# Attention operands filled up to 128 rows, values at columns 0 and 96, and the heads' norms split between VectorE and GpSimd

## The chip, the core and the metric

The kernel runs on one core of one Trainium2 chip. A core has a matrix engine (TensorE, PE in the profile; its weight loads are listed apart as PEld and overlap the matmuls), VectorE (DVE), ScalarE (ACT), GpSimd (POOL) and SyncE (SP), which here only issues DMAs. Each engine works through its own instructions in order, and semaphores tie the engines together. The metric is the device time of one launch in microseconds, as the median of several runs. A change of less than about 0.3% can't be told from none.

## The reference

One layer of a trunk in which three kinds of heads stand side by side: 2048 tokens, width 1024, all in float32.

```python
h = RMSNorm(x); z = h @ W_in + b_in      # columns shared out among the heads
y = concat[ FoX attention (8 heads of 64), mLSTM (4), HGRN2 (4) ]
x = x + y @ W_out
h = RMSNorm(x)
x = x + W_down( silu(conv3(h W_up)_gate) * conv3(h W_up)_up )
```

What the change touches is the attention. Its score of query t and key u, with q and k normed and c the running sum of the log forget gates, is

```python
s = einsum('qd,kd->qk', q, k) / 8 + c[q] - c[k]     # per head
s = where(kpos <= qpos, s, -inf)
o = softmax(s) @ v
y_head = RMSNorm(o) * gain                          # norm over the 64 columns of a head
```

## The kernel before, in words

**Numbers.** A matmul here takes operands of reduced precision (type fp32r). To come near float32, an operand is split into a high part and the low part that is left over, and three matmuls are added up: high by high, high by low, low by high. The helper `mm3` (L198) does this in the projections.

**Stages.** The kernel first makes the projections z and, woven into them, the mLSTM and HGRN2 mixers, in two halves of 1024 tokens. For the attention these write to HBM: the high and low parts of q and k, transposed, with one row for each column of the heads (s_qh, s_ql, s_kh, s_kl); the values (s_v), 130 numbers for a token and head, which are 64 high parts, a one, 64 low parts and a zero; the forget sums (s_fc), and rows of ones and zeros (s_one). The last projections end with stores of s_v and s_qh by GpSimd's queue (L321, L404). Then come the attention, the output projection with the second norm (`phase_out`) and the FFN (`ffn_up`, `ffn_down`), whose large products are made of fewer products of blocks with sums of blocks on VectorE and GpSimd.

**Who sets the order.** Outside the attention's loop a planner of the framework puts the instructions of each engine in order, by a simulated time and by what each one depends on. The loop of the attention stands in `with k.tc.manual_schedule()` (L1006): there each engine keeps the order in which the program names its instructions. Memory is shared between stages: QB and KB of the even heads lie where the first buffer of the projections' high parts was, QA and KA of the even heads where the first buffer of their low parts was, those of the odd heads in the second buffers, and V of the even heads where the low parts of the projection's weights (wlo) were.

**Operands of a head.** `att_load` (L805) issues a head's loads on SyncE, all through one helper (L813), so that all carry its line. QB is 64 rows of the high parts of q and six rows more: four that receive the negated row maxima, and two with ones; KB has the high parts of k, four rows of ones or zeros against the maxima, and two rows of the forget sums. So one matmul with 70 rows gives the high product, plus the forget sums, minus the maximum of the row. QA is q high over q low and KA is k low over k high, 128 rows, so that one more matmul gives both cross products. V is a tile of 128 tokens by 16 by 130.

**The loop.** For each of the 8 heads there are 4 blocks of 512 queries, and for each of them the key tiles of 128 up to the diagonal: 4 + 8 + 12 + 16 = 40 steps for a head. In a step:

- `att_scores` (L876) makes the scores transposed, keys by queries: the matmul with QB and KB (L885), the one with QA and KA (L886), and on the diagonal a mask added by a matmul with the identity. ScalarE makes the exponentials pf (L892) and their high part ph (L894); the low part pl (L898) is a subtraction, in three steps of four on GpSimd, in the fourth on VectorE one step later.
- `att_maxima` (L829) runs ahead, 12 pieces before the first score and then 22: a matmul with QB and KB the other way round (L845), a mask, and a maximum over the row on VectorE (L850). When a block of 512 queries is through, its maxima are transposed and written into rows 64 to 67 of QB (L863).
- `att_values` (L903) runs three steps behind the scores (`SKEW`): V high by ph with the ones column, whose output row 64 is the sum of the softmax (L911), V low by ph (L912), and V high by pl (L913), all added into one PSUM tile. At the end of a block the sum goes through ScalarE and TensorE (transposes) into the tile `o` of the head, with tokens on the rows.
- In the fourth step of each head from the second on, the loads of the head after it are issued.

**A head's norm.** `att_finish` (L937) hands the pieces of a head's norm to `Later` (L787), a list of due steps: `put(n, f)` runs f at the end of the n-th step from now, behind that step's other work. For heads 0 to 6 one norm covers all 16 tiles of 128 tokens and falls into the head after it. From its step 6 on come the reciprocal of the softmax sums (rl), the squares on ScalarE and their totals on VectorE, four tiles a step. In step 11 come two products of the totals with rl (L960, L961) and the start of the inverse root in `rms_steps` (L113): three operations with a constant, then the first of three Newton steps. The other two follow in steps 12 and 13:

```python
nc.vector.tensor_tensor(u, out, out, op=ALU.mult)
nc.vector.tensor_tensor(u, u, h, op=ALU.mult)
nc.vector.scalar_tensor_tensor(out, u, 1.5, out, op0=ALU.add, op1=ALU.mult)
```

All of these work on 128 x 16 numbers. From step 15 the factor is multiplied by rl (L970), and then four tiles a step are multiplied by it on VectorE (L971) and by the gain on GpSimd (L976). SyncE stores the head's columns into s_y (L981). The last head has no head after it: each of its four blocks of queries is normed by itself (128 x 4 numbers), beginning four steps after the block's end.

**Beside it.** The load of the gains `ga` (L1628) belongs to the attention and stands ahead of the loop in the program. The weights of the output projection are loaded and split inside the loop (L1040). `phase_out` reads s_y back by tiles of 128 tokens, all heads together.

## Time and profile before

| | before |
|---|---|
| median of 3 runs | 2932.36 us (2932.19 to 2941.21) |
| the profiled execution | 2937.63 us |
| its span, first to last instruction | 2935.5 us |
| mean granted clock of TensorE | 0.977 |
| TensorE busy | 2817.4 us, 96% of the span |
| VectorE busy | 2005.9 us, 68% |
| GpSimd busy | 1435.1 us, 49% |
| ScalarE busy | 1280.0 us, 44% |

By stage, in us of the span:

| stage | from, to | TensorE busy | VectorE | ScalarE | GpSimd | clock |
|---|---|---|---|---|---|---|
| projections and mixers | 0 to 939 | 880.89 | 596.28 | 278.12 | 373.70 | 0.97 |
| attention | 939 to 1440 | 467.65 | 381.69 | 381.91 | 339.73 | 0.95 |
| output projection | 1440 to 1680 | 227.64 | 129.10 | 74.60 | 40.65 | 0.96 |
| FFN | 1680 to 2935.5 | 1241.22 | 898.81 | 545.33 | 681.07 | 1.00 |

How to read the lines that follow. A line in order of time has the start and the duration in us (with x3 behind it, the sum of three), the engine, the program line, the operation, out<-in by the program's names, shapes, and in brackets how long the engine had waited and for whom. SPq and POOLq are the queues of SyncE and GpSimd, which issue DMAs. A line of the waits names who waited and for whom, then the sum in us, the number of waits and the longest. A line of the stretches has from and to and the length, the busy time of TensorE, its weight loads, VectorE, ScalarE and GpSimd with their instructions, then the granted clock, the share of the DMA engines and GB/s. A line of a group has the busy time and the mean of one instruction in ns, and the idle time ahead of them with what ended most of it.

### The profile page before, as it was taken

To read this page: it belongs to the slowest core of one execution; us is meant where nothing else is said; L and a number is where in the kernel's file an instruction comes from. 1 tells how busy PE (TensorE), PEld (TensorE's weight loads), DVE (VectorE), ACT (ScalarE), POOL (GpSimd) and SP (SyncE) were. 2 spreads that over 40 slices of the span, in tenths; PEclk is the share of its full clock that TensorE was granted. 3 is DMA by queue.
4 is the path that set the end of the run, shared out by engine and by line. 5 is a ranking of instruction groups with operands and counts; after the bars stand their busy time and mean duration, and the time that the engine had idled before them with its cause. 6 is when DMAs were issued, how large, how long until landed. Compare 5 with 4: busy or idle time off the path is not lost. (4 is left out here: it accounts for less than half of the span.)

```text
span 2935.5 us, 42833 instructions
## 1 busy us (share of the span) xinstructions
PE 2817.4 (96%) x15181; PEld 2342.7 (80%) x15181; DVE 2005.9 (68%) x3384; ACT 1280.0 (44%) x2167; POOL 1435.1 (49%) x1199
## 2 busy tenths in 40 slices
PE   7999988999988999999899899999999999999999
PEld 7898987889988666666688788888788888888887
DVE  7337687265786787778546577677797577777655
ACT  4213323132322778878424344444454343444443
POOL 2245452334454577766302366666475644444443
PEclk9999997999999999999999999999999999999999
DMA  4424434333334554342257444444777333333666
GB/s 159 127 93 133 150 96 143 94 108 97 111 107 143 107 114 88 81 92 49 72 179 246 148 155 151 154 148 158 268 247 271 114 108 108 108 105 117 232 214 209
DMA packets 346615, 411.07 MB, mean 140 GB/s; under 512 B 47650, under 2 KB 234096, under 8 KB 343232
## 3 DMA queue, kind: packets, MB, share of 16 engines
q1 hardware_dynamic: 292016, 318.45, 37.2%
q10 hardware_dynamic: 51952, 81.45, 7.6%
q0 software_dynamic: 2432, 8.42, 0.8%
q8 instruction: 120, 1.97, 0.3%
q14 instruction: 95, 0.78, 0.1%
HBM read 280.24 MB, written 127.98 MB: 139 GB/s over the span
## 5 line engine op out<-in xcount | busy, mean ns | idle before, releaser
L1221 POOL TENSOR_TENSOR w<-w,w 128x512 fp32r<-128x512 f32 x302 | 404.8, 1353 | 403.3 <-ACT w L1220 339.2
L1409 PE MATMUL ps<-w,w 128*128 128x512 f32 x1848 | 420.9, 389 | 4.0 <-ACT w L1400 2.0
L1409 PEld LDWEIGHTS ps<-w,w 128*128 128x128 f32 x1848 | 346.6, 188 | 77.6 <-ACT w L1400 2.4
L198 PE MATMUL w<-whi,hhi 128*128 128x256 f32 (+1 forms) x1280 | 370.4, 289 | 3.1 <-DVE lr L1766 2.0
L198 PE MATMUL w<-whi,hlo 128*128 128x256 f32 (+1 forms) x1280 | 371.3, 290 | 0.0
L198 PE MATMUL w<-wlo,hhi 128*128 128x256 f32 (+1 forms) x1280 | 370.4, 290 | 0.6 <-POOL wlo L189 0.6
L898 POOL TENSOR_TENSOR pl<-pf,ph 128x512 fp32r<-128x512 f32 (+2 forms) x240 | 287.8, 1212 | 146.6 <-ACT ph L894 133.3
L1402 POOL TENSOR_TENSOR w<-w,w 128x512 fp32r<-128x512 f32 x154 | 216.3, 1412 | 200.9 <-ACT w L1400 155.4
L1220 ACT ACTIVATE w<-w 128x512 fp32r<-128x512 f32 x302 | 180.4, 627 | 258.7 <-POOL w L1221 86.7
L850 DVE TENSOR_REDUCE mx<-m 128x1 f32<-128x512 f32 (+2 forms) x320 | 190.8, 605 | 91.3 <-PE m L845 63.1
L1401 DVE TENSOR_TENSOR w<-w,w 128x512 fp32r<-128x512 f32 x154 | 179.9, 1178 | 103.4 <-ACT w L1399 102.0
L198 PEld LDWEIGHTS w<-whi,hhi 128*128 128x128 f32 x1280 | 245.2, 192 | 4.8 <-issue 3.8
L198 PEld LDWEIGHTS w<-wlo,hhi 128*128 128x128 f32 x1280 | 244.9, 191 | 2.7 <-POOL wlo L189 1.0
L198 PEld LDWEIGHTS w<-whi,hlo 128*128 128x128 f32 x1280 | 244.7, 191 | 1.8 <-issue 0.5
L892 ACT ACTIVATE pf<-s 128x512 f32<-128x512 f32 (+1 forms) x320 | 172.5, 539 | 91.1 <-PE s L886 50.9
L1226 DVE TENSOR_TENSOR w<-w,w 128x512 f32<-128x512 f32 x176 | 149.8, 870 | 85.3 <-DMA w<-in_w_up_dram 81.0
L189 POOL TENSOR_TENSOR wlo<-wraw,whi 128x1024 fp32r<-128x1024 f32 (+1 forms) x56 | 135.3, 2433 | 111.7 <-ACT whi L188 102.2
L894 ACT ACTIVATE ph<-pf 128x512 fp32r<-128x512 f32 (+1 forms) x320 | 185.1, 578 | 10.3
L1267 DVE SCALAR_TENSOR_TENSOR u<-ps,fcol,u 128x1023 f32<-128x1023 f32 x88 | 108.9, 1279 | 95.3 <-ACT u L1266 95.3
L913 PE MATMUL pv<-pl,V 128*65 128x512 f32 (+1 forms) x320 | 121.7, 380 | 25.2 <-DVE pl L898 24.3
L1400 ACT ACTIVATE w<-w 128x512 fp32r<-128x512 f32 x154 | 96.6, 628 | 111.3 <-PE ps L1409 88.7
L1399 ACT ACTIVATE w<-w 128x512 fp32r<-128x512 f32 x154 | 95.9, 623 | 89.8 <-POOL w L1402 44.4
(374 smaller groups left out, 7092.1 us busy)
## 6 DMA issues: line engine op xcount, KB each, us to landing
w<-in_w_up_dram SPq DMA_DIRECT2D x182, 256.0 KB
w<-s_g SPq DMA_DIRECT2D x154, 256.0 KB
w<-in_w_down_dram SPq DMA_DIRECT2D x110, 256.0 KB
wraw<-in_w_in_dram SPq DMA_DIRECT2D x48, 512.0 KB
s_g<-u ACTq DMA_DIRECT2D x88, 256.0 KB
w<-s_w SPq DMA_DIRECT2D x88, 256.0 KB
s_g<-w ACTq DMA_DIRECT2D x66, 256.0 KB
x<-in_x_dram SPq DMA_DIRECT2D x32, 512.0 KB
```

The lines of the kernel that those rows point to most:

```text
L189: nc.gpsimd.tensor_tensor(lo[:, q : q + n, :], raw, h.bitcast(F32), op=ALU.subtract)
L198: nc.tensor.matmul(out, lsl(lhs[a], i), rsl(rhs[b], i), start=(i == 0 and j == 0), stop=(i == n - 1 and j == 2))
L850: nc.vector.tensor_reduce(mx[:, i, kb : kb + 1], m[:, 0:n], axis=AX.X, op=ALU.max)
L892: nc.scalar.activation(pf[:, c0:], s[:, c0:], AF.Exp)
L894: nc.scalar.activation(ph[:, c0:], pf[:, c0:], AF.Copy)
L898: eng.tensor_tensor(pl[:, c0:], pf[:, c0:], ph[:, c0:].bitcast(F32), op=ALU.subtract)
L1220: nc.scalar.activation(h, t, AF.Copy)
L1221: nc.gpsimd.tensor_tensor(lo, t, h.bitcast(F32), op=ALU.subtract)
L1226: nc.vector.tensor_tensor(t, x, y, op=op)
L1401: nc.vector.tensor_tensor(gl, gr, gh.bitcast(F32), op=ALU.subtract)
L1402: nc.gpsimd.tensor_tensor(wl, wr, wh.bitcast(F32), op=ALU.subtract)
L1409: nc.tensor.matmul(tiles[tile], g[x][:, tile * P : (tile + 1) * P], w[y], start=j == 0 and c == 0, stop=j == nj - 1 and c == 2,)
```

## The change

It has four parts.

**128 rows.** The matmuls L845 and L885 take all 128 rows of QB and KB instead of 70. For this QB and KB are no longer made anew for each head: there are two pairs, made once ahead of the loop, and GpSimd fills their rows 64 to 127 with zeros. The call for the first pair, `zero(0)`, stands ahead of the hand-ordered block, the one for the second, `zero(1)`, in it, behind the first head's loads. The loads of ones and forget sums then write rows 64 to 69 as before.

**Columns of V.** The tile has 160 columns for a token tile instead of 130, with the low parts from column 96 on instead of 65 (96 x 4 bytes = 384 = 3 x 128; 160 x 4 = 640 = 5 x 128). The zero column is no longer loaded. High and low parts are loaded by a DMA each, so V takes four DMAs instead of two.

**Order of the loads.** The first part of V was loaded ahead of QA and KA; now all of V comes behind them.

**The norm.** The two products with rl, the three Newton steps and the product of the factor with rl go from VectorE to GpSimd. A Newton step has four operations there instead of three. The three operations with a constant at its start stay on VectorE. In the last head the quarters begin 18, 10, 4 and 4 steps after their blocks' ends instead of 4 each, and they share one tile of 128 x 16 x 64 for the squares and products, where before each had its own of two.

```diff
+VL, VW = 96, 160
...
-def rms_steps(k, pool, out, ss, n, epsf, tag):
+def rms_steps(k, pool, out, ss, n, epsf, tag, pool_too=False):
...
     for _ in range(3):
         yield
+        if pool_too:
+            nc.gpsimd.tensor_tensor(u, out, out, op=ALU.mult)
+            nc.gpsimd.tensor_tensor(u, u, h, op=ALU.mult)
+            nc.gpsimd.tensor_scalar(out=u, in0=u, scalar1=1.5, scalar2=None, op0=ALU.add)
+            nc.gpsimd.tensor_tensor(out, out, u, op=ALU.mult)
+            continue
...
@@ def att_load(k, h, st):
-    QA, KA, QB, KB = (k.t(k.pat[f"{t[1]}{h % 2}"], [P, T], F32R, tag=t) for t in ("QA", "KA", "QB", "KB"))
-    V = k.t(k.pat[f"V{h % 2}"], [P, 16, 130], F32R, tag="V")
+    QA, KA = (k.t(k.pat[f"A{h % 2}"], [P, T], F32R, tag=t) for t in ("QA", "KA"))
+    QB, KB = k.qkb[h % 2]
+    V = k.t(k.pat[f"V{h % 2}"], [P, 16, VW], F32R, tag="V")
...
     ld(KB[68:70], k.s_fc[h])
-    v = k.s_v[:, h, :].rearrange("(jt p) c -> p jt c", p=P)
-    ld(V[:, 0:4], v[:, 0:4])
     ld(QA[0:64], k.s_qh[r])
     ld(QA[64:128], k.s_ql[r])
     ld(KA[0:64], k.s_kl[r])
     ld(KA[64:128], k.s_kh[r])
-    ld(V[:, 4:16], v[:, 4:16])
+    v = k.s_v[:, h, :].rearrange("(jt p) c -> p jt c", p=P)
+    for j in (slice(0, 4), slice(4, 16)):
+        ld(V[:, j, 0:65], v[:, j, 0:65])
+        ld(V[:, j, VL : VL + 64], v[:, j, 65:129])
...
-                        m[:, 0:nn], QB[0:70, q0 : q0 + P], KB[0:70, kb * BLK : kb * BLK + nn], start=True, stop=not last
+                        m[:, 0:nn], QB[:, q0 : q0 + P], KB[:, kb * BLK : kb * BLK + nn], start=True, stop=not last
...
-    nc.tensor.matmul(s[:, c0:], KB[0:70, js], QB[0:70, qs], start=True, stop=False)
+    nc.tensor.matmul(s[:, c0:], KB[:, js], QB[:, qs], start=True, stop=False)
...
-    nc.tensor.matmul(po[0:64, c0:], V[:, j, 65:129], ph[:, c0:], start=False, stop=False)
+    nc.tensor.matmul(po[0:64, c0:], V[:, j, VL : VL + 64], ph[:, c0:], start=False, stop=False)
...
-        att_finish(k, st, pa, 4 * qb, 4, later, 4)
+        att_finish(k, st, pa, 4 * qb, 4, later, (18, 10, 4, 4)[qb])
...
@@ def att_finish: first()
-        w["sq"] = k.t(pa, [P, n, HD], tag=f"asq{n}", bufs=bufs)
+        if n == 16 or "sq" not in st:
+            st["sq"] = k.t(pa, [P, 16, HD], tag="asq", bufs=1)
+        w["sq"] = st["sq"][:, t0 : t0 + n, :]
...
     def scale():
-        nc.vector.tensor_tensor(w["ss"], w["ss"], w["rl"], op=ALU.mult)
-        nc.vector.tensor_tensor(w["ss"], w["ss"], w["rl"], op=ALU.mult)
+        nc.gpsimd.tensor_tensor(w["ss"], w["ss"], w["rl"], op=ALU.mult)
+        nc.gpsimd.tensor_tensor(w["ss"], w["ss"], w["rl"], op=ALU.mult)
...
-        w["chain"] = rms_steps(k, pa, w["s"], w["ss"], HD, 1.0, f"a{n}")
+        w["chain"] = rms_steps(k, pa, w["s"], w["ss"], HD, 1.0, f"a{n}", pool_too=True)
...
         if c.start == 0:
-            nc.vector.tensor_tensor(w["s"], w["s"], w["rl"], op=ALU.mult)
+            nc.gpsimd.tensor_tensor(w["s"], w["s"], w["rl"], op=ALU.mult)
...
@@ def attention(k, pa, ps, side):
+    k.qkb = [[k.t(k.pat[f"B{i}"], [P, T], F32R, tag=t) for t in ("QB", "KB")] for i in range(2)]
+    def zero(i):
+        for x in k.qkb[i]:
+            k.nc.gpsimd.memset(x[64:128].bitcast(F32), 0.0)
+
+    zero(0)
     with k.tc.manual_schedule():
         att_load(k, 0, sts[0])
+        zero(1)
         att_load(k, 1, sts[1])
```

## The prediction

> **What bounds the kernel now.** I read the page first, then the stretches by stage, the waits of TensorE and the order of time at three places. The attention runs from 939 to 1440 us. TensorE has little idle time anywhere, so what counts is where it waits and where its clock falls.
>
> ```profile
> span 2935.5 us, 42833 instructions
> ```
> ```profile
> 943.10:963.60 20.50, 13.71 (x42) 8.91 (x42) 10.43 (x21) 4.97 (x11) 5.91 (x10) 0.50 0.90 247
> ...
> 1042.00:1045.50 3.50, 3.50 (x10) 2.12 (x10) 3.29 (x8) 1.23 (x2) 2.77 (x4) 0.52 0.00 0
> ...
> 1400.00:1411.00 11.00, 6.99 (x23) 3.96 (x22) 10.00 (x21) 4.08 (x8) 7.63 (x9) 0.69 0.15 36
> ```
> ```profile
> PE pv L913 <- DVE pl L898: 24.3, 15, 4.0
> ```
> The stretches give, behind the five busy times, the granted clock, the DMA share and GB/s. At the start of the attention the clock is 0.50 for 20.5 us. After a wait of TensorE it is about half for a stretch such as 1042 to 1045.5, which costs half of those 3.5 us. In all of the attention TensorE waits 24.3 us for the low parts (pl) that VectorE makes, nearly all of it in eight long waits, one behind each head's end and a second one in the last head. With the clock lost behind them I count 24 + 8 x 1.75 = 38 us. That is the most that the steps on GpSimd could win. The profiled execution took 2937.63 us, 2.1 more than its span, and the median of the runs is 2932.36. I work out differences in the span and add them to the median.
>
> **Loads of the first head: values last, and the zeroed rows.** SyncE's order of time, and its wait:
>
> ```profile
> 916.20 0.51 SPq L1628 DMA_DIRECT2D ga<-in_out_g_dram  x1
> ...
> 918.90 0.26 SPq L813 DMA_DIRECT2D KB<-s_fc  x1
> 939.18 0.39 SPq L813 DMA_DIRECT2D V<-s_v  x1
> ...
> 941.45 0.85 SPq L813 DMA_DIRECT2D KA<-s_kh  x1
> ```
> ```profile
> SPq L813 <- PE w L198: 20.0, 1, 20.0
> ```
> ```profile
> 939.06 0.28 PE L845 MATMUL m<-KB,QB 70*128 70x256 f32 x1
> ...
> 946.82 0.78 PE L885 MATMUL s<-QB,KB 70*128 70x512 f32 x1
> 953.71 0.79 PE L886 MATMUL s<-QA,KA 128*128 128x512 f32 x1 [6.11 <-DMA KA<-s_kh]
> ```
> V's first load waits 20 us for the projection's last matmul, whose memory it takes, and the four loads of QA and KA stand behind it. So the first score, begun at 946.82, gets its second pair at 953.71. With V moved past those four loads they would go at 919, and 953.71 - 946.82 = 6.9 us would be won. But the load of ones into QB[64:70] now waits for the memset of QB's rows 64 to 127, and everything behind it on SyncE (KB's rows, QA, KA, V, the next head's loads) waits with it. When does GpSimd come to that memset?
>
> ```profile
> 904.27 0.59 POOL L321 DMA_DIRECT2D s_v<-h  x1 [0.30 <-POOL h L318]
> ```
> ```profile
> 936.92 0.68 POOL L318 TENSOR_TENSOR h<-z,h 128x256 fp32r<-128x256 f32 x1
> ...
> 940.79 0.71 POOL L404 DMA_DIRECT2D s_qh<-h  x1 [0.35 <-ACT h L317]
> ...
> 950.73 0.10 POOL L315 MEMSET h<- 128x4 f32 x1 [6.58 <-DMA s_qh<-h]
> ...
> 951.89 1.11 POOL L321 DMA_DIRECT2D s_v<-h  x2
> 956.06 1.27 POOL L898 TENSOR_TENSOR pl<-pf,ph 128x512 fp32r<-128x512 f32 x1 [3.07 <-ACT ph L894]
> ```
> ```profile
> s_qh<-h POOLq DMA_DIRECT2D x4, 256.0 KB, 2.8
> ```
> ```profile
> L1578 POOL MEMSET q<- 128x1024 f32 x1 | 1.0, 951 | 0.3 <-POOLq L1807 0.3
> ```
> The zeroing of the first pair stands outside the hand-ordered block, so the planner may put it early. The one instruction with the same place in the program is the load of ga: it needs nothing but an input, yet it was issued at 916.20, behind SyncE's last load of the projections, and GpSimd's first attention step (956.06) stands behind its last store of the projections (951.89). I take it that the memsets come behind that store too. Then SyncE issues no QA or KA loads while the store of 940.79 is under way, and I let it land after its median 2.8 us, at 943.6, before GpSimd asks for it (950.73 - 6.58 = 944.15). From 950.73 to the store's end, 951.89 + 1.11 = 953.00, are 2.3 us, so GpSimd is free at 946.4. A memset of 1024 columns took 0.951 us, so 2048 columns take 1.9 and the pair 3.8: 950.2. The loads of ones and of the forget sums follow and land some 2.8 us on (the store's time as the nearest row), at 953. TensorE's first maximum thus begins 14 us late. The maxima ahead of the first score took 946.82 - 939.06 = 7.8 us, bound by VectorE; they end at 960.8. QA and KA, 2.1 MB issued from 950.8, need 8.5 us at the 247 GB/s of the stretch above, 1.5 more to begin: 960.8 as well. Against 953.71 that is **+7 us**. Bounds: -6.9 if the memsets come early; +14 if the store lands as late as it did before. The second pair's memsets (3.8 us on GpSimd) lie ahead of its first pl, which has nothing to work on by then; without that cover they cost 3.8, inside the upper bound. V goes in four loads, not two: 0.39 us of issue each on a queue that is idle, and V is read three steps after the first score; uncovered, its 260 KB cost 1.1 us at 247 GB/s. Later heads load 35 steps ahead.
>
> **The heads' norms, first seven heads.** A head's end at 1205 to 1220 us, VectorE, GpSimd and TensorE in order of time:
>
> ```profile
> 1210.12 0.18 DVE L132 SCALAR_TENSOR_TENSOR as<-a16u,as 128x16 f32<-128x16 f32 x1
> ...
> 1211.02 0.80 DVE L130 TENSOR_TENSOR a16u<-as 128x16 f32<-128x16 f32 x1
> ...
> 1213.11 1.22 DVE L132 SCALAR_TENSOR_TENSOR as<-a16u,as 128x16 f32<-128x16 f32 x1
> ...
> 1215.94 0.81 DVE L970 TENSOR_TENSOR as<-as,rl 128x16 f32<-128x16 f32 x1
> ...
> 1218.22 1.74 DVE L898 TENSOR_TENSOR pl<-pf,ph 128x512 fp32r<-128x512 f32 x1
> ```
> ```profile
> 1210.27 4.02 POOL L898 TENSOR_TENSOR pl<-pf,ph 128x512 fp32r<-128x512 f32 x3 [1.94 <-ACT ph L894]
> 1215.42 1.29 POOL L898 TENSOR_TENSOR pl<-pf,ph 128x512 fp32r<-128x512 f32 x1 [1.13 <-ACT ph L894]
> ...
> 1217.97 1.44 POOL L898 TENSOR_TENSOR pl<-pf,ph 128x512 fp32r<-128x512 f32 x1
> ```
> ```profile
> 1213.21 0.40 PE L886 MATMUL s<-QA,KA 128*128 128x512 f32 x1
> 1213.45 0.40 PE L845 MATMUL m<-KB,QB 70*128 70x512 f32 x1
> ...
> 1217.27 0.39 PE L912 MATMUL pv<-ph,V 128*64 128x512 f32 x1
> 1220.02 0.69 PE L913 MATMUL pv<-pl,V 128*65 128x512 f32 x1 [2.36 <-DVE pl L898]
> ```
> Alone, a step of the norm takes VectorE 0.18 us; beside GpSimd's pl it takes 0.80 to 1.22, until GpSimd's instruction ends. So the factor of the norm (L970) is ready at 1216.75; VectorE's products and its own pl follow, and TensorE, ready at 1217.5, waits until 1220.
>
> Now the 15 steps of the norm go to GpSimd, twelve of them four by four behind pl of steps 12, 13 and 14, then the last factor. Call one p. GpSimd starts at 1210.27, makes three pl of 1.29 and 13 small ones: the factor is ready at 1214.14 + 13p. VectorE's products wait for it, and its pl stands behind two of them, as before. If VectorE gets in ahead of GpSimd's next pl, product 0.4, reduce 0.65 (covered by that pl, 1.29 from the product on), product 0.35, one gain 0.7 and pl 0.65 follow: 3.05 us, and TensorE waits 13p - 0.3. If GpSimd's pl goes first, 1.29 and 0.3 more are in the way: 13p + 1.3. Before it was 2.5.
>
> p isn't in the trace. From 0.68 us at 256 columns and 1.29 at 512 follows 0.11 at 16 columns; 0.10 for the 128x4 memset says the same. Each step needs the one before, and GpSimd took 0.30 us to begin an instruction on its own result (904.27). So p lies between 0.11 and 0.43; I take 0.22, nearer the low end, because that 0.30 was before a DMA issue. Then TensorE waits 2.55 or 4.15, 3.35 in the mean: **0.9 more than before in each of seven heads, +6 us**. Bounds: p = 0.11 with VectorE first shortens each wait to 1.1 and the clock may hold, -3.2 a head, -22; p = 0.43 with the mean, +3.6 a head, +25.
>
> [...]
>
> **The last head.** Its quarters are normed one by one. Two long waits stand here:
>
> ```profile
> 1395.25 0.33 PE L913 MATMUL pv<-pl,V 128*65 128x256 f32 x1 [3.04 <-DVE pl L898]
> ...
> 1405.11 0.69 PE L913 MATMUL pv<-pl,V 128*65 128x512 f32 x1 [4.01 <-DVE pl L898]
> ```
> The first quarter now begins at step 24 of the head instead of 10, so the second wait (4.0, and 3.4 of the eleven us at clock 0.69) goes: -7. But the second quarter begins at step 24 too, so GpSimd gets eight small steps (8 x 0.22 = 1.8 us) beside a pl of 1.29 in steps of five matmuls, 5 x 0.235 = 1.2 us. Over three such steps it falls 5.6 us behind with some 2.5 us of slack, so TensorE waits about 3 again, and 1.75 for its clock; the first wait grows by 0.9. Sum: **-1, taken as 0**; bounds -6 and +6. The stores of these quarters come at step 33, seven steps (8 us) before the end, and the output projection's first load needs them then; hidden by the last scores, +4 if not.
>
> **128 rows and V's columns: 0.** The matmuls and their number stay.
>
> ```profile
> L885 PEld LDWEIGHTS s<-QB,KB x320: 187/188/353, 946.7 to 1436.6; 70*128 70x128 f32 x160
> ```
> ```profile
> L886 PEld LDWEIGHTS s<-QA,KA x320: 189/191/336, 953.7 to 1436.8; 128*128 128x128 f32 x160
> ```
> ```profile
> L1409 PE MATMUL ps<-w,w 128*128 128x512 f32 x1848 | 420.9, 389 | 4.0 <-ACT w L1400 2.0
> ```
> Weights of 70 and 128 rows load alike (least, median and longest in ns), and the full-row L886 takes 0.24 us to the next start, as the 70-row L845 does. The FFN's matmuls take 420.9 / 1848 = 0.228. If that gap of 0.007 came from rows and columns, some 1700 matmuls would win 12 us: bounds -12 and 0, and I take 0, because L886 has full rows already. Memory moves by 2 KB a head buffer, which no row prices.
>
> **Sum:** +7 + 6 + 0 + 0 = +13, so 2932.4 + 13 = 2945.
>
> **The rivals.**
> *Zeroing early.* The planner puts the first memsets into GpSimd's idle time before 939. For it: the wait of 6.58 and others leave room, and QB's memory was free at 917. Against it: ga. Start -6.9 instead of +7: 2931.
> *The norm gets off VectorE's back (the other side: faster).* The place is the factor's arrival at 1214.14 + 13p, and it decides below p = 0.12, with VectorE getting in first. Waits shrink to about 1.1 us, and I let the clock hold; -22 in seven heads, -6 in the last, start +7: 2911. For it: the 0.10 us memset; against it: each step waits for its predecessor.
> *GpSimd's small steps are dear*, p = 0.35: 13p makes +2.6 a head, +18; last head +5, start +7: 2962.
> *Full rows hold the clock.* The half-clock stretches (14 us behind eight waits, some 5 at the start) go: 2945 - 19 = 2926. For it: 20.5 us at 0.50 while TensorE was mostly on 70-row work; against it: no row ties the clock to rows. [...]
>
> **How the numbers follow.** The forecast has 0.48, with its own range 2936 to 2960. Early zeroing has 0.18, the relief 0.16, the dear steps 0.12, the clock 0.06. About 0.3% (8.8 us) is what a measurement of this kernel tells from no change, so 2923.6 and 2941.2 are the limits. Faster: 0.03 of early zeroing, 0.14 of the relief, 0.03 of the clock, 0.20. Same: 0.10 of the forecast, 0.12 of early zeroing, 0.02 and 0.03, 0.27. Slower: the rest, 0.53. The range 2914 to 2966 leaves out most of the relief and the far end of the dear steps, some 0.17.
>
> **What would show it.** Right: the first maximum near 953 behind two memsets of about 1.9 us, SyncE's load of ones waiting for GpSimd, no wait of TensorE for KA over 2 us; steps of 128x16 on GpSimd at 0.1 to 0.3; waits for pl of 2 to 4 us at every head's end, with half clock behind them. Wrong: memsets before 939 with QA issued by 925; waits for pl under 1.5 us; matmul starts 0.228 us apart.

## The result, and the profile after

| | before | after |
|---|---|---|
| median | 2936.60 us (4 runs) | 2955.68 us (4 runs) |
| ratio | 1 | 1.0075, 95% interval 1.0056 to 1.0093 |
| the profiled execution, its span | 2937.63, 2935.5 us | 2955.15, 2953.4 us |

So the change makes the kernel slower by 0.75%, about 22 us; a second comparison of the same two kernels (first experiment below) gave 1.0079. The forecast was 2945.0, 13 us slower, with its own range 2936 to 2960. Direction and range hold; the sum is 9 us short. (A fourth run moved the median of the kernel before from 2932.36 to 2936.60.) In the last experiment below, one of six executions took 7051 us; its time and ratio are those of the other five.

To see where it went, the table follows seven marks on TensorE in the profiled executions: (a) the last transposition of the projections, (b) the second score matmul of the first step, (c) the same matmul of step 10 of head 0, (d) that of step 10 of the last head, (e) the last transposition of the attention, (f) the first product of the FFN and (g) its last. These are marks b to f of the changed kernel, in order of time:

```profile
958.38 0.77 PE L896 MATMUL s<-QA,KA 128*128 128x512 f32 x1 [2.33 <-DMA KA<-s_kh]
...
975.56 0.28 PE L896 MATMUL s<-QA,KA 128*128 128x256 f32 x1
...
1396.03 0.28 PE L896 MATMUL s<-QA,KA 128*128 128x256 f32 x1
...
1459.64 0.46 PE L935 MATMUL x<-ident,oT 65*128 65x65 f32 x4 [0.68 <-ACT oT L929]
...
1662.79 0.47 PE L1273 MATMUL ps<-b11h,w 128*128 128x512 f32 x1
```

All times are in us. The stretch c to d holds the norms of heads 0 to 5 and d to e those of heads 6 and 7, because a head's norm falls into steps 11 to 18 of the next one. For e the last of its four transpositions counts.

| kernel | a | a to b | b to c | c to d | d to e | e to f | f to g |
|---|---|---|---|---|---|---|---|
| before | 938.47 | 15.23 | 19.02 | 413.55 | 54.80 | 205.57 | 1282.58 |
| after | 934.47 | 23.91 | 17.18 | 420.47 | 63.85 | 202.90 | 1284.28 |
| difference | -4.0 | +8.7 | -1.8 | +6.9 | +9.05 | -2.7 | +1.7 |

Up to a and from f on both kernels run the same work; those two columns differ by 6 us and more among the kernels of this study, which is the scatter of single executions. In the attention the stretches are steadier, but not exact: moving V's loads alone changed c to d by 0.15 us, while the changed kernel run a second time took 423.14 there instead of 420.47. So a difference of less than about 3 us in c to d is not read as an effect below.

**The start** of the changed kernel, in order of time on SyncE, GpSimd and TensorE, and the wait of SyncE:

```profile
943.95 0.30 SPq L822 DMA_DIRECT2D QB<-s_one  x1
945.69 0.27 SPq L822 DMA_DIRECT2D KB<-s_one  x1
...
946.31 0.45 SPq L822 DMA_DIRECT2D QA<-s_qh  x1
...
948.08 0.59 SPq L822 DMA_DIRECT2D KA<-s_kh  x1
```
```profile
940.98 1.11 POOL L329 DMA_DIRECT2D s_v<-h  x2
942.13 1.80 POOL L1023 MEMSET QB<- 64x2048 f32 x1
943.87 1.80 POOL L1023 MEMSET KB<- 64x2048 f32 x1
```
```profile
948.45 0.55 PE L855 MATMUL m<-KB,QB 128*128 128x256 f32 x1 [13.23 <-DMA KB<-s_fc]
```
```profile
SPq L822 <- POOL QB L1023: 29.9, 1, 29.9
```

The memsets stand right behind the last store of the projections, and SyncE waits 29.9 us for the first of them, with all but the first two loads of the first head behind it.

**A head's end.** GpSimd, VectorE and TensorE of the changed kernel, at the same head as in the prediction:

```profile
1217.65 1.29 POOL L908 TENSOR_TENSOR pl<-pf,ph 128x512 fp32r<-128x512 f32 x1 [1.44 <-ACT ph L904]
1218.90 0.21 POOL L130 TENSOR_TENSOR a16u<-as 128x16 f32<-128x16 f32 x1
1219.19 0.22 POOL L131 TENSOR_TENSOR a16u<-a16u,a16h 128x16 f32<-128x16 f32 x1
1219.50 0.25 POOL L132 TENSOR_SCALAR a16u<-a16u 128x16 f32<-128x16 f32 x1
1219.84 0.22 POOL L133 TENSOR_TENSOR as<-as,a16u 128x16 f32<-128x16 f32 x1
1220.02 1.30 POOL L908 TENSOR_TENSOR pl<-pf,ph 128x512 fp32r<-128x512 f32 x1
...
1224.87 0.22 POOL L983 TENSOR_TENSOR as<-as,rl 128x16 f32<-128x16 f32 x1
1225.05 1.27 POOL L908 TENSOR_TENSOR pl<-pf,ph 128x512 fp32r<-128x512 f32 x1
```
```profile
1225.13 1.48 DVE L984 TENSOR_TENSOR asq<-ao,as 128x256 f32<-128x256 f32 x1 [4.63 <-POOL as L983]
1226.53 0.68 DVE L860 TENSOR_REDUCE mx<-m 128x1 f32<-128x512 f32 x1
1227.13 0.56 DVE L984 TENSOR_TENSOR asq<-ao,as 128x256 f32<-128x256 f32 x1
1227.61 1.74 DVE L908 TENSOR_TENSOR pl<-pf,ph 128x512 fp32r<-128x512 f32 x1
```
```profile
1223.73 0.45 PE L923 MATMUL pv<-pl,V 128*65 128x512 f32 x1 [0.64 <-POOL pl L908]
...
1229.41 0.69 PE L923 MATMUL pv<-pl,V 128*65 128x512 f32 x1 [3.81 <-DVE pl L908]
```

A small step takes GpSimd 0.21 to 0.25 us, but they start 0.29 to 0.34 apart, since each needs the one before; two that do not need each other started 0.15 apart in the last head, at 1427.39 and 1427.54. Four of them put the next pl off by 1.12 us. VectorE waits 4.63 us for the factor, with its own pl behind that wait, and TensorE waits 0.64 and 3.81 us where it had waited 2.36.

**The last head**, TensorE, VectorE and GpSimd:

```profile
1431.97 0.45 PE L923 MATMUL pv<-pl,V 128*65 128x512 f32 x1 [1.51 <-POOL pl L908]
...
1435.23 0.69 PE L923 MATMUL pv<-pl,V 128*65 128x512 f32 x1 [1.88 <-POOL pl L908]
...
1438.49 0.69 PE L923 MATMUL pv<-pl,V 128*65 128x512 f32 x1 [0.86 <-POOL pl L908]
...
1444.43 0.69 PE L923 MATMUL pv<-pl,V 128*65 128x512 f32 x1 [3.55 <-DVE pl L908]
```
```profile
1442.37 1.20 DVE L122 TENSOR_SCALAR a4m<-ass 128x4 f32<-128x4 f32 x1 [2.58 <-POOL ass L974]
...
1443.68 0.69 DVE L908 TENSOR_TENSOR pl<-pf,ph 128x512 fp32r<-128x512 f32 x1
```
```profile
1427.10 0.21 POOL L973 TENSOR_TENSOR ass<-ass,rl 128x4 f32<-128x4 f32 x1
...
1430.66 1.26 POOL L908 TENSOR_TENSOR pl<-pf,ph 128x512 fp32r<-128x512 f32 x1
```

Twelve small steps of two quarters, from 1427.10 to 1430.66, hold one pl back by 3.6 us; then the third quarter's totals stand in GpSimd's queue behind a pl, and VectorE's pl behind the wait for them. The stretches of time give the price in clock (behind the five busy times: granted clock, DMA share, GB/s):

```profile
1433.80:1447.50 13.70, 7.86 (x18) 4.44 (x18) 3.17 (x8) 4.12 (x7) 11.93 (x28) 0.50 0.20 59
```

### The profile page after: what moved, and what is told of

Its sections match the earlier page's. It is cut to its first block, busy times and chain, and to the rows that moved or that the text cites. A ratio compares the mean times of both kernels' runs of the same rounds, so it can differ in the third digit from the quotient of the medians.

```text
span 2953.4 us, 42896 instructions
## 1 busy us (share of the span) xinstructions
PE 2809.3 (95%) x15181; PEld 2332.7 (79%) x15181; DVE 1964.4 (67%) x3252; ACT 1279.4 (43%) x2167; POOL 1476.8 (50%) x1368
## 5 line engine op out<-in xcount | busy, mean ns | idle before, releaser
L1241 ACT ACTIVATE w<-w 128x512 fp32r<-128x512 f32 x302 | 180.4, 627 | 256.8 <-POOL w L1242 85.7
L1421 ACT ACTIVATE w<-w 128x512 fp32r<-128x512 f32 x154 | 96.7, 628 | 116.7 <-PE ps L1430 88.5
L855 PE MATMUL m<-KB,QB 128*128 128x512 f32 (+2 forms) x320 | 130.3, 414 | 14.6 <-DMA KB<-s_fc 13.2
```

The source lines that it names most:

```text
L1241: nc.scalar.activation(h, t, AF.Copy)
```

## The experiments

Each kernel was run beside the kernel before; ratios are against it, with 95% intervals. The stretches are those of the table above.

**The changed kernel again.** No edit.

> The changed kernel once more, beside the runs of this set. Both theories: 18 to 24 us slower than before (22 in the first comparison, 17.5 between the two profiled executions, of which the projections, the same instructions in both, took 4 us less).

Measured 2961.38 us against 2936.74, ratio 1.0079 (1.0066 to 1.0092), +23 us. Stretches: a to c 41.2 against 34.25, c to d 423.14, d to e 64.10. As expected.

**The norms back on VectorE.** The changed kernel with

```diff
-        nc.gpsimd.tensor_tensor(w["ss"], w["ss"], w["rl"], op=ALU.mult)
-        nc.gpsimd.tensor_tensor(w["ss"], w["ss"], w["rl"], op=ALU.mult)
+        nc.vector.tensor_tensor(w["ss"], w["ss"], w["rl"], op=ALU.mult)
+        nc.vector.tensor_tensor(w["ss"], w["ss"], w["rl"], op=ALU.mult)
...
-        w["chain"] = rms_steps(k, pa, w["s"], w["ss"], HD, 1.0, f"a{n}", pool_too=True)
+        w["chain"] = rms_steps(k, pa, w["s"], w["ss"], HD, 1.0, f"a{n}")
...
-            nc.gpsimd.tensor_tensor(w["s"], w["s"], w["rl"], op=ALU.mult)
+            nc.vector.tensor_tensor(w["s"], w["s"], w["rl"], op=ALU.mult)
```

> The changed kernel with the norms' steps back on VectorE (due times of the last head as changed). Theory: GpSimd's small steps cost the changed kernel +7 us in seven heads and about +10 in the last, the late zeroing +5 to +8 at the start, rows and columns nothing; so about 5 to 8 us slower than the kernel before, and the changed kernel's other 15 us are gone. Rival (operands: the full rows or V's columns and extra DMAs cost something in every head): still 15 us or more slower than before.

Measured 2937.31, ratio 1.0006 (0.9995 to 1.0018): +2 us, not to be told from none. The theory's 5 to 8 was too high, the rival's 15 is out. In sum, the norms on GpSimd are the loss: without them the later start (a to c 40.02 against 34.25) is balanced by the stretch c to d, which took 407.44, 6 us less than before the change. The operands seem to win something that I had at nothing.

**Only the last head's norms back on VectorE.**

```diff
-        w["chain"] = rms_steps(k, pa, w["s"], w["ss"], HD, 1.0, f"a{n}", pool_too=True)
+        w["chain"] = rms_steps(k, pa, w["s"], w["ss"], HD, 1.0, f"a{n}", pool_too=n == 16)
...
+        e = nc.gpsimd if n == 16 else nc.vector
```

> The changed kernel with only the last head's four small norms back on VectorE. Theory (GpSimd falls behind in the last head, up to twelve small steps in one loop step): 8 to 12 us faster than the changed kernel, about 10 to 14 slower than before; no wait of TensorE for a low part over 1 us in the last 25 us of the attention but those that the last head had before. Rival (it is the due times of the last head, two quarters in the same step, not the engine): no more than 3 us faster than the changed kernel.

Measured 2953.10, ratio 1.0062 (1.0046 to 1.0078). That is 2.6 and 8.3 us faster than the two medians of the changed kernel and, by the ratios, 4 to 5, so less than the theory's 8 to 12; the intervals of these ratios overlap. The stretch d to e is the cleaner reading: 57.50 against 63.85 and 64.10, so the four small norms cost 6.4 us on GpSimd. But the theory's sign, no wait over 1 us in the last 25 us of the attention, failed: one of 4.09 us stands at 1436.97. Two quarters in the same step, the rival's cause, make VectorE late too. The rest of that stretch's loss is the large norm of head 6, which falls into it.

**V behind QA and KA alone.** The kernel before with its two V loads moved behind KA.

```diff
-    v = k.s_v[:, h, :].rearrange("(jt p) c -> p jt c", p=P)
-    ld(V[:, 0:4], v[:, 0:4])
...
     ld(KA[64:128], k.s_kh[r])
+    v = k.s_v[:, h, :].rearrange("(jt p) c -> p jt c", p=P)
+    ld(V[:, 0:4], v[:, 0:4])
     ld(V[:, 4:16], v[:, 4:16])
```

> The kernel before with both loads of V behind QA and KA, nothing else. Theory: QA and KA are issued by 920 instead of after 939, the first score's second matmul no longer waits (6.1 us before), 6.9 us faster: about 2929.5 against 2936.6. Rival (the end of the projections and the maxima set the pace, and the time is lost again at the first read of V): within 2 us of before.

Measured 2930.57, ratio 0.9984 (0.9974 to 0.9995), -5 us. The stretches show 27.76 us from a to c instead of 34.25, -6.5, and nothing elsewhere in the attention: the 6.9 of the prediction within half a us.

**128 rows alone.** The kernel before with the zeroed pairs and full rows.

```diff
-                        m[:, 0:nn], QB[0:70, q0 : q0 + P], KB[0:70, kb * BLK : kb * BLK + nn], start=True, stop=not last
+                        m[:, 0:nn], QB[:, q0 : q0 + P], KB[:, kb * BLK : kb * BLK + nn], start=True, stop=not last
...
-    nc.tensor.matmul(s[:, c0:], KB[0:70, js], QB[0:70, qs], start=True, stop=False)
+    nc.tensor.matmul(s[:, c0:], KB[:, js], QB[:, qs], start=True, stop=False)
...
+    k.qkb = [[k.t(k.pat[f"B{i}"], [P, T], F32R, tag=t) for t in ("QB", "KB")] for i in range(2)]
...
```

> The kernel before with the zeroed pairs and 128 rows alone; V's first load ahead of QA as before, norms on VectorE. Theory: the two memsets stand behind the last projection's store on GpSimd, the load of ones waits for them, and the first score's second matmul comes 8 to 9 us later: +6 to +9 us, all of it before the tenth step of the first head. Rival (full rows cost time in each matmul): +0.007 us or more for each of 1700 matmuls, 12 us or more beside the start; rival (full rows hold the clock up): the half-clock stretches behind the heads' ends are gone and it is 8 us or more faster than the theory says.

Measured 2938.53, ratio 1.0014 (1.0005 to 1.0022), +4 us, below the theory's 6 to 9. The start has the expected loss (a to c 42.34, +8.1), but c to d took 408.00, -5.6. A small part belongs to the matmuls: ten undisturbed steps at a head's beginning take 13.09 us in the mean instead of 13.17, and ten at its end 13.93 instead of 14.03, which makes 1.2 us for the fourteen such tens between c and d. The larger part is clock. Between c and d the granted clock was 0.50 for 27.3 us before and for 13.7 us with 128 rows alone, which costs 6.8 us less, while the waits of TensorE for pl grew from 17.2 to 19.5 us. These are ten steps over the same head's end before, with 128 rows alone, and with the norms on VectorE, which has 128 rows too, as stretches of time:

```profile
1086.70:1104.70 18.00, 15.18 (x73) 10.53 (x72) 16.08 (x37) 12.85 (x26) 12.58 (x12) 0.91 0.64 135
```
```profile
1089.80:1106.20 16.40, 13.56 (x72) 9.36 (x72) 15.54 (x32) 12.67 (x26) 11.57 (x11) 1.00 0.68 147
```
```profile
1091.30:1109.20 17.90, 15.03 (x72) 10.39 (x72) 15.96 (x37) 12.81 (x26) 12.62 (x12) 0.90 0.63 118
```

The waits of TensorE in the three stretches, in the same order:

```profile
PE pv L913 <- DVE pl L898: 2.8, 1, 2.8
```
```profile
PE pv L914 <- DVE pl L899: 2.8, 1, 2.8
```
```profile
PE pv L923 <- DVE pl L908: 2.9, 1, 2.9
```

The waits are alike. The clock fell behind it in two and not in the third, and one of the two has full rows. What differs is where the wait fell. In the traces of before and after the granted clock changes only on a grid of 3.413 us: the 33 changes of the one and the 37 of the other all lie within 0.005 us of it. These are the window of that grid that holds most of the wait, and the one behind it, before; then the two windows that share the wait, and the one behind them, with 128 rows alone:

```profile
1093.32:1096.74 3.42, 1.28 (x6) 0.97 (x7) 3.32 (x8) 0.70 (x2) 1.72 (x2) 1.00 1.18 256
1096.74:1100.15 3.41, 3.41 (x9) 2.35 (x8) 3.14 (x10) 2.50 (x5) 0.40 (x1) 0.50 0.19 73
```
```profile
1093.69:1097.10 3.41, 2.01 (x12) 1.29 (x11) 3.31 (x8) 2.90 (x5) 2.79 (x4) 1.00 1.04 153
1097.10:1100.51 3.41, 1.98 (x9) 1.52 (x10) 3.27 (x11) 1.12 (x2) 1.01 (x1) 1.00 1.04 285
1100.51:1103.93 3.42, 3.42 (x21) 2.27 (x20) 3.39 (x7) 2.86 (x6) 1.61 (x2) 1.00 0.03 12
```

Before, TensorE idled 2.14 us of one window, and the next ran at half clock. With 128 rows alone it idled 1.40 and 1.43 us of two, and the clock stayed. The same count over the traces of before and after from c to d: each of the 11 windows at full clock with 1.96 us of idling or more was followed by half clock, and none of the 217 with 1.74 or less. From the start to g the line is less sharp: of the 29 with 1.81 or more 28 were followed by half clock, of the 1603 with less six. Five of the 11 are the changed kernel's, so full rows do not hold the clock, and in this stretch how much clock a wait cost hung on where it fell on the grid. That differs between executions: the two of the changed kernel had 20.5 and 30.7 us at half clock from c to d. The kernels with 70 rows and packed norms on VectorE (before, V behind QA and KA alone, V's columns) had 27.3 us each, those with 128 rows (this one, the norms back on VectorE, the late zeroing) 13.7, 17.1 and 20.5; whether the rows have a share in that, by moving the waits on the grid, is not shown. Nor did this head keep what it won: VectorE came late a second time, by 1.41 us, and the ten steps behind took 15.75 us instead of 14.18.

**The norm alone.** The kernel before with GpSimd's steps, the shared tile and the last head's due times; 70 rows, 130 columns, V first. Its edit is the norm part of the change.

> The kernel before with the norm part of the change alone: GpSimd's steps and the last head's due times; 70 rows, 130 columns, V first. Theory: seven heads with waits of 3.5 to 4 us instead of 2.5, +9 to +14; last head +8 to +11, output projection -3: 14 to 22 us slower than before. Rival (it is the operands beside GpSimd's steps that cost it): less than 8 us slower.

Measured 2961.96, ratio 1.0085 (1.0072 to 1.0098), +25 us, a little above the expected 14 to 22. The start is that of before (34.34); c to d took 425.34, +11.8 for six norms, and d to e 65.24, +10.4. The cost is GpSimd's, whatever the operands.

**Zeros by loads.** The norms on VectorE, and the zeros read from a row of zeros in HBM instead of set by GpSimd.

```diff
+    if h < 2:
+        for x in (QB, KB):
+            ld(x[70:128], k.s_one[0:1].broadcast_to([58, T]))
     ld(QB[64:70], k.s_one[0:6])
...
-    zero(0)
```

> The changed kernel with the norms on VectorE, and rows 70 to 127 of the two pairs filled by SyncE's loads from a row of zeros instead of GpSimd's memsets. Theory (at the start everything waits for memsets that stand behind the last projection's store): the first score's second matmul comes 13 to 15 us earlier than with the norms on VectorE alone, which stood at +1.4 us against before; so 11 to 14 us faster than before, about 2923. Rival (the end of the projections holds the loads, whoever writes the zeros): within 3 us of +1.4.

A miss: 2944.52, ratio 1.0033 (1.0020 to 1.0046) and, by the ratios, 8 us slower than without this edit. The waits of SyncE in the profile, and the issue of the load that the first one is for:

```profile
SPq L822 <- DMA QB<-s_one: 13.7, 1, 13.7
SPq L822 <- DMA KB<-s_one: 13.5, 1, 13.5
```

```profile
914.65 0.45 SPq L822 DMA_DIRECT2D QB<-s_one  x1
```

The first of the loads of zeros was issued at 914.65, as the theory had it, but the two of 464 KB were so slow that SyncE stood behind each of them for over 13 us; the first score's second matmul came 27.8 us after the projections, and head 1's maxima waited for the second pair again. Why they were so slow is not shown: no run tried another row count, or another source than one row. So this kernel said nothing on the theory; the late zeroing below does.

**Small steps spread over the loop.** On top of the zeros by loads: the norms of heads 0 to 6 on VectorE with one small step in a loop step, and the last head's quarters in tiles of their own again.

```diff
+            nc.vector.tensor_tensor(u, out, out, op=ALU.mult)
+            yield
+            nc.vector.tensor_tensor(u, u, h, op=ALU.mult)
+            yield
+            nc.vector.scalar_tensor_tensor(out, u, 1.5, out, op0=ALU.add, op1=ALU.mult)
...
-    for _ in range(4):
+    for _ in range(13 if n == 16 else 4):
         later.put(i, link)
         i += 1
```

> The kernel with zeros by loads and norms on VectorE, in which the large norms of heads 0 to 6 issue one small step in each loop step instead of three (the quarters of the last head have their own tiles again). Theory (at a head's end three or more small steps of VectorE in one loop step, each stretched by GpSimd's subtraction beside it, make pl late): the waits of 2 to 3 us at each head's end go, with the clock behind them; 12 to 25 us faster than with three in a step. Rival (the products of 128x256 and the gains, not the small steps, make the wait): within 4 us of it.

Measured 2947.44, ratio 1.0035 (1.0023 to 1.0047): no faster than three in a step, as the rival's number has it. But the heads did gain: c to d 400.84 against 415.40, -14.6. It was lost from e to f, 218.91 against 202.53. TensorE in that stretch:

```profile
1441.85 1.97 PE L1107 MATMUL ty<-ident,yin 128*128 128x128 f32 x8 [12.18 <-DMA yin<-s_y]
```

The output projection waits 12.18 us for its first load, which stands behind the last head's last store. The next kernel shows the reason.

**V's columns and four loads alone.** The kernel with V behind KA, and beside that

```diff
-    V = k.t(k.pat[f"V{h % 2}"], [P, 16, 130], F32R, tag="V")
+    V = k.t(k.pat[f"V{h % 2}"], [P, 16, VW], F32R, tag="V")
...
+    for j in (slice(0, 4), slice(4, 16)):
+        ld(V[:, j, 0:65], v[:, j, 0:65])
+        ld(V[:, j, VL : VL + 64], v[:, j, 65:129])
```

> The kernel before with V behind QA and KA and, beside that, V's 160 columns and four loads; 70 rows, norms on VectorE. Theory (columns and the extra loads cost and win nothing): as with V last alone, 4 to 7 us faster than before, each stage within 1 us of it. Rival (pieces of 256 and 260 bytes land late, or aligned columns read faster): a start more than 2 us later, or more than 0.05 us in each ten steps.

Another miss: 2950.28, ratio 1.0026 (1.0015 to 1.0036), where the same without the columns stood at 0.9984. The attention is untouched: a to c 26.85 against 27.76, c to d 413.55 against 413.40. All of it lies from e to f, 220.68 against 205.69:

```profile
1441.96 1.97 PE L1089 MATMUL ty<-ident,yin 128*128 128x128 f32 x8 [11.98 <-DMA yin<-s_y]
```

It is the same wait as in the spread kernel, and the memory map of the programs tells why. The output projection's pool begins at byte 143,296 of each partition. The pool with the attention's working tiles ends at 143,216 before the change. One V tile lies below it, and its 30 more columns by 16 tiles by 4 bytes push the end to 145,136: now the first tile of the output projection (yin) overlaps the last tiles of that pool, among them the quarters' squares that the last stores read, and is loaded only when those are done. In the changed kernel the shared tile of the squares gives 2 KB back, and the pool ends at 143,088. The spread kernel had V's columns and separate tiles, so it overlapped too. These two are the only kernels with that overlap and the only ones with the long wait; the wider columns with the shared tile took 201 to 203 us from e to f in every kernel here.

**Late zeroing.** The norms on VectorE; head 0 on 70 rows, and the first pair zeroed in head 1 for head 2.

```diff
+    if h == 2:
+        later.put(1, lambda: zero(QB))
+        later.put(5, lambda: zero(KB))
+        later.put(5, rows)
...
+            R = 128 if st["h"] else 70
```

> The changed kernel with the norms on VectorE, and head 0 on 70 rows, so that the first pair is zeroed by GpSimd only in head 1 (steps 3 and 7) for head 2; the other seven heads have 128 rows. Theory (the start costs 7 us because the first loads wait for memsets behind the last projection's store): first score's second matmul 9 us after the end of the projections instead of 24; from there as with the norms on VectorE; 12 to 14 us faster than that kernel (+1.4 against before), 9 to 13 faster than before. Rival (V behind QA and KA, or the second pair's memsets, hold the start): at most 4 us faster than before.

Measured 2930.11, ratio 0.9964 (0.9952 to 0.9977), -11 us: as the theory has it. From a to b it took 8.91 us, the same as with V last alone, against 23.69 with the early memsets.

**Late zeroing and spread steps.** On top of it, the norms of heads 0 to 5 with one small step in a loop step, all on VectorE; heads 6 and 7 as they were.

```diff
+    slow = n == 16 and st["h"] < AH - 2
...
+    for _ in range(13 if slow else 4):
```

> The kernel with the late zeroing, in which the norms of heads 0 to 5 issue one small step of VectorE in each loop step (those of heads 6 and 7 stay as they were, so that the output projection finds its rows in time). Theory (three and more stretched small steps in one loop step make pl late at a head's end): about 2.5 us for each of six heads, 12 to 15 us faster than the late zeroing alone and 22 to 28 us faster than before, the attention's heads 1 to 6 at 42.5 to 43 us instead of 45. Rival (what is won in the heads is lost again behind the attention, as with all seven spread): within 4 us of the late zeroing.

Measured 2909.58, ratio 0.9894 (0.9878 to 0.9909): 31 us faster than before, the fastest kernel of the study, and 21 faster than the late zeroing alone, more than the theory's 12 to 15. c to d took 390.47, 18.9 less than there; e to f 201.44. (The expectation's 42.5 to 45 us leave out a head's first ten steps, 13.1 us. Heads 1 to 6 took 55.96 in the mean here, 59.10 with the late zeroing alone, 59.79 before and 60.99 after the change, which is 42.9, 46.0, 46.7 and 47.9.) From c to d:

```profile
968.30:1358.70 390.40, 383.31 (x2073) 262.42 (x2073) 313.28 (x606) 332.53 (x630) 298.52 (x252) 1.00 0.45 90
```

The waits of TensorE fell from 17.4 to 7.0 us in this stretch, and the half clock behind them, 20.5 us with the late zeroing alone, is gone. The theory's 2.5 us for each head were the waits alone.

**The same spread, on GpSimd.** Heads 0 to 5 do their two-operand steps on GpSimd again, one in a loop step.

```diff
-            nc.vector.tensor_tensor(u, out, out, op=ALU.mult)
+            nc.gpsimd.tensor_tensor(u, out, out, op=ALU.mult)
             yield
...
-    for _ in range(13 if slow else 4):
+    for _ in range(15 if slow else 4):
```

> The kernel with the late zeroing in which the norms of heads 0 to 5 do their two-operand steps on GpSimd as in the change, but one small step in each loop step instead of four; heads 6 and 7 on VectorE. Theory (the change loses in the heads because four steps of 0.28 us stand together behind one subtraction; GpSimd has about 1.3 us free in four loop steps): heads 1 to 6 at 42.5 to 44 us instead of 47 as changed, 20 to 28 us faster than before, within 8 us of the same spreading on VectorE. Rival (any step of the norm on GpSimd delays its low parts, however spread): heads 1 to 6 at 46 us or more, less than 14 us faster than before.

Measured 2918.29, ratio 0.9921 (0.9902 to 0.9940), -23 us, as the theory has it. c to d took 401.25: 19.2 less than in the changed kernel, where four steps stand together, and 10.8 more than with VectorE. Heads 1 to 6 took 57.75, less the first ten steps 44.6, just outside the expected 44. But spreading won as much with VectorE, 18.9 us (409.33 to 390.47), so the packing costs either engine the same and is not what the change added. The move to GpSimd is: it costs 13.0 us with packed steps (420.47 against 407.44) and 10.8 with spread ones. How much of that is the engine, and how much its longer chain, which takes three loop steps more in the spread kernel, these runs do not separate.

## Why the prediction was right, and where not

The difference from a to g by terms, with the rows of the experiments as the way between before and after:

| term | predicted | measured | from |
|---|---|---|---|
| start, a to c | +7 | +6.8 | 41.09 against 34.25 |
| norms of seven heads | +6 | +14.5 | c to d, 420.47 against 408.00 with 128 rows alone: +12.5 for six; d to e, 57.50 against 55.52: +2.0 for the seventh |
| last head's quarters | 0 | +6.4 | d to e, 63.85 against 57.50 |
| 128 rows | 0 | -5.6 | c to d, 408.00 against 413.55 |
| rest of d to e, and e to f | | +0.7 - 2.7 | 55.52 against 54.80; 202.90 against 205.57 |
| sum | +13 | +20.1 | |

The two profiled executions differ by 17.8 from start to g: these 20.1, -4.0 in the projections and +1.7 in the FFN.

**Start: right in each step, and in size by step 10.** That the memsets come behind the last projection's store was read from where ga was issued; they stood there, at 942.13 with projections that ended 4 us earlier, against 946.4 predicted. A memset took 1.80 us (1.9), the first maximum came at 948.45 (953 less 4), and the late zeroing took the term away. At the first score's second matmul the loss was 8.7 us: QA and KA took 12.1 us from their first issue at 946.31, not the 10.0 counted (the 1.5 of it for a beginning was my estimate, and no row shows it), and TensorE waited 2.33 us for KA, over the 2 that I had named. By step 10 it was 6.8, the +7 forecast. That it would be -6.9 with V last and nothing else came out too, at -6.5. The rival of early zeroing was wrong.

**Norms of seven heads: right mechanism, mis-sized.** "Call one p ... I take 0.22" is the step that failed first: the first pl in the rows above starts at 1217.65 and the factor is done at 1225.09, three pl of 1.25 in between, so 13 p = 3.7 and p = 0.28. I had taken the busy time, and 0.07 to 0.09 us between two dependent steps were missing. That is 0.8 us of the 1.2 that a head cost more than forecast. The waits for pl show the same: 29.2 us from c to d against 17.3 with the norms on VectorE, 2.0 more in each of six heads, not 0.9. The other part is "product 0.4 ... and pl 0.65": I let VectorE get in first and then counted its steps as if alone, but beside GpSimd's pl the product took 1.48 and its own pl 1.74, where a pl of the same size took 0.69 in the last head, at 1443.68, with no pl of GpSimd beside it. From the factor to the end of that pl 4.26 us passed, where the two cases of the prediction had 3.05 and 4.64, 3.85 in the mean. The rival of dear steps, +18 with p = 0.35, was nearer the measured +14.5 than my +6, though its p was too high.

**Last head: wrong by 6 us.** "TensorE waits about 3 again, and 1.75 for its clock" failed. I let GpSimd fall behind by eight small steps in each of three loop steps; the first of these has twelve, and I counted nothing for the third quarter, whose totals VectorE waits for with its pl behind (the 3.55 us). The four waits of the fence make 7.8 us, and the clock stayed at 0.50 for 13.7 us instead of 3.5. The -7 for the moved quarters failed too. With the norms back on VectorE and the quarters as moved, two of them still meet in one step, and a wait as long stands there instead:

```profile
1421.44 0.44 PE L923 MATMUL pv<-pl,V 128*65 128x512 f32 x1 [4.09 <-DVE pl L908]
```

That kernel took 55.52 us from d to e, and 128 rows alone with the old due times 55.48. So the due times win nothing, and GpSimd's steps cost 6.4 on top.

The tail that I feared (+4) was none: e to f became 2.7 shorter, since TensorE ran at half clock behind e before and doesn't now, as the stretches behind e of before and after show:

```profile
1441.50:1448.30 6.80, 5.79 (x15) 4.43 (x16) 4.21 (x20) 1.01 (x2) 0.73 (x1) 0.50 0.22 77
```
```profile
1459.90:1466.70 6.80, 5.59 (x29) 4.40 (x28) 2.02 (x8) 1.01 (x2) 3.05 (x15) 1.00 0.21 77
```

**Rows: within the bounds, the wrong end.** "I take 0, because L886 has full rows already" missed 0.08 to 0.10 us in ten steps; the rest is clock, which hung on where the waits fell on the grid and so may be luck of the executions. The rival that full rows hold the clock is out: behind the waits that fell into one window it came down with full rows too (in the changed kernel TensorE stood still from 1225.6 to 1229.0, and from there to 1232.4 the clock was 0.50). This gain hid half of what the norms cost, so that c to d came out at +6.9 against my +6 for the wrong reason. "Memory moves by 2 KB a head buffer, which no row prices" was the most dangerous sentence: by itself it costs 15 us, and only the shared tile, which I read as a side matter, pays for it.

**Relief of VectorE, the faster rival: wrong**, for p is over its limit of 0.12. But the place was the right one: beyond the 11 us of the late zeroing, spreading the steps of six heads thinly wins some 20 us on VectorE, by the ratios, and still some 12 with the steps on GpSimd.

## What to carry to other kernels

Where several engines work in a hand-written order, small dependent steps cost not their busy time but their spacing (here 0.29 to 0.34 us on GpSimd, where a step was busy 0.21 to 0.25), times how many stand in one step of the loop ahead of something that TensorE waits for; spread them one to a step before moving them to another engine: here that won 19 us from c to d on either engine, while the move cost 11 to 13. A memset at the start belongs where its engine is free and its readers are not all waiting; here it could be left out for the first head. And a tile that grows by 2 KB can cost 15 us far away from its use, as here from e to f: compare where the next stage's memory begins.

## What was not expected of the hardware

GpSimd's dependent steps of 128 x 16 took 0.21 to 0.25 us and started 0.29 to 0.34 apart. Full rows made ten steps of the attention 0.08 to 0.10 us shorter at equal instructions (13.09 against 13.17, and 13.93 against 14.03). A wait of TensorE of 2.8 us was followed by half clock in one kernel and by full clock in another, at the same place and with equal work: where the clock fell 2.14 us of it lay in one window of a grid of 3.413 us, where it stayed 1.40 and 1.43 in two. Loads of 464 KB to 58 rows from one row in HBM held their queue for 13.7 and 13.5 us, where four loads of 512 KB to 64 rows were issued at 946.31 to 948.08 in the changed kernel and the last of them was there for the matmul at 958.38.
